# Large SBUF pages of a one-core encoder layer moved to multiples of 128 bytes

## The chip, the cores and the metric

The kernel runs on one core of one Trainium2 chip. The metric is the device time of one execution in microseconds. Three runs of the kernel before took 1744.45 to 1746.06 us, 1745.98 in the median. The core has a matrix engine (TensorE, called PE in the profile, with its weight loads shown apart as PEld), a vector engine (VectorE, DVE), an activation engine (ScalarE, ACT), a general engine (GpSimd, POOL) and a queue engine (SyncE, SP) that here only issues DMA transfers. SBUF is the memory on the core from which the engines read: 128 partitions, each with its own run of bytes. A tile of shape [128, n] lies at the same byte address in every partition. PSUM is where PE writes its results.

## The reference, cut to what matters

One layer (DEPTH = 1) of a bidirectional encoder over 1024 positions of 1024 features, all in float32:

```python
h = _rmsnorm(x, attn_norm_w[layer])
proj = jnp.einsum("bsd,de->bse", h, w_in)         # 8192 columns: GLU input, q, v, z_f, z_b, og, g_a, g_b
a = jax.nn.glu(glu_in); a = _dwconv_centred(a, dw_w, dw_b)     # 31 taps
a = jnp.einsum("bsc,cd->bsd", jax.nn.silu(_layernorm(a, ln_w, ln_b)), pw_w)
o = _bi_hgrn2(q, v, z_f, z_b, lb[0], lb[1])       # gated scan in both directions, 8 heads of 128
bmix = jnp.einsum("bse,ed->bsd", norm(o) * jax.nn.silu(og), o_w)
y = jax.nn.sigmoid(g_a) * a + jax.nn.sigmoid(g_b) * bmix
x = x + jnp.einsum("bsd,de->bse", y, w_out[layer])
gate, val = jnp.split(jnp.einsum("bsd,df->bsf", _rmsnorm(x, ffn_norm_w), w_up), 2)
x = x + jnp.einsum("bsf,fd->bsd", jax.nn.silu(_dwconv_centred(gate, ...)) * val, w_down)   # 2816 wide, 3 taps
return _rmsnorm(x, final_norm_w)
```

Most of the arithmetic is in the large products: with `w_in`, `hgrn_o_w`, `w_out`, `ffn_w_up` and `ffn_w_down`.

## The kernel before

**Matmuls.** All large products are made of one kind of matmul: a weight block of 128x128 stays in the array while 512 columns of activations move through it (the moving operand is a page of 128x512 elements, 2048 bytes in each partition). To keep float32 precision, every operand is split into a high part in the rounded type fp32r and a low part (line 124: ACT casts the high part, then DVE subtracts it for the low part). A product is then three matmuls, on lines 148 to 150: high by high, high by low, low by high. Each matmul has its own weight load. Products with `w_in` and with `ffn_w_up` save an eighth of the work: two output columns by two halves of the sequence are computed with seven products in place of eight (`pair_job`, in the order 1, 2, 6, 7, 5, 4, 3), which need sums and differences of the activations (made once) and of the weights. A pair of columns is 7 products of 12 matmuls, 84 in all.

**Weight sums.** In `pair_job` the weight rows come into a page `wr` (two buffers), the other columns into `sw`. Where no stored sums exist, GpSimd issues DMA transfers that add in flight: into `sw` from memory (`G.dma_start(o, a, accum_op=ALU.add)`, line 301), then from `sw` into `wr`, then within `wr`. In the feed-forward `sw` has one buffer, so its next load (lines 374 and 375, issued on SP's queue) waits until it has been read. The first three feed-forward columns use sums stored earlier and do without.

**Order.** PE's instructions run in the order in which the program writes them. The other engines' instructions are put in order by a planner with a cost model, except a few that are pinned. Side work is interleaved by hand with counts of pieces (a piece is six matmuls), for example 1.67 pieces of projection behind each tap of the 31-tap convolution on DVE (line 1037).

**Stages**, by the profile's time: norm and gated input to 87 us; the convolution on DVE beside input projections to about 335; the rest of the projections and the layer norm to about 478; the scan of eight heads beside the remaining projections to about 870; output of the scan and `w_out` to about 1088; the up projection of the feed-forward (22 columns) to about 1493; the down projection to 1697; the final norm and the stores.

**Where the tiles lie.** Pools of tiles are stacked in SBUF: a pool that is released gives its space to the next. Within a pool tiles follow each other, each rounded up to 32 bytes. Below all lie 16512 bytes and the pool of constants, which ends at 19488. So the start of a page depends on everything below it. These are the starts modulo 128 before the change (first page in brackets; all pages of a row have the same remainder unless two are given):

| pool | tiles | start mod 128 before |
|---|---|---|
| main (from 19488) | `tm` `wr` `wp` `hx` `ev` | 32 |
| gp0 (123936), p0, p1 (140832) | `gl` `ch`; `xt` `xn`; `su` `hy` `sw` `w` `wq` `ca` | 32 |
| heads (123936) | `none`, 64 bytes | 32 |
| heads (124000) | `q` `f` `kG` `zi` `qF` `D` `A` `tb` | 96 |
| heads (193568), behind three `Tt` of 64 bytes | `Sf` `Sb` `S` `v` `kT` `jk` `og` | 32 |
| fw (123936), p4 (148512) | `h` (named `h7`) `rs` `sw`; `mg` `x2` `xq` | 32 |
| fu (148512) | two `gp` of 4104 bytes | 32 and 64 |
| fu (156768) | `ft` `w` (named `w4`) `su` `wq` `hy` | 96 |
| fd (123936), fs (194848), fy | `xr` `gx`; `sr` `wq` `su`; `y` | 32 |

`ident`, the identity matrix that the transposes use as moving operand, starts at 16512, a multiple of 128. In the up projection the seven products take their operands from pages of different remainders: products 1, 2 and 6 move `hx` pages (32) against `wp` weights (32); product 7 moves `h` pages (32) and product 5 `hx` pages (32) against `wq` weights (96); product 4 moves `hy` (96) against `wq` (96); product 3 moves `hy` (96) against `wp` (32).

## Time and profile before

| what | us |
|---|---|
| median of three runs | 1745.98 |
| the profiled execution | 1742.35 |
| its span, first to last instruction | 1740.5 |
| PE busy in the span | 1711.8 (98%) |
| DVE busy | 1254.2 (72%) |
| ACT busy | 828.0 (48%) |
| DMA, mean rate over the span | 177 GB/s |

The granted clock of PE was 0.998 of full speed over the execution. A row of the profile's groups reads: line, engine, operation, tile written and tiles read, shapes, count, then the group's busy time, the mean duration of one in ns, and the idle time of its engine just before them with what ended it. Matmuls overlap each other, so the mean duration of one (some 390 ns) is not what one costs; the distance from start to start is. Windows cut the span into stretches and give each engine's busy time and its number of instructions in each.

### The profile page before, as it was taken

What the parts mean: (1) busy time and instruction counts of PE and PEld (TensorE: products, weight loads), DVE (VectorE), ACT (ScalarE), POOL (GpSimd) and SP (SyncE); (2) the same over time, 40 slices, a digit from 0 to 9 for tenths busy, and PEclk for the clock granted to TensorE, in tenths of its full rate; (3) what the DMA queues carried; (4) which work ended last, traced back from release to release, by engine and by line L of the source; (5) the groups of instructions that cost most, each with busy time, mean ns of one, the idle gap of its engine ahead of it and who ended that gap; (6) DMA issues with size and microseconds to landing.
All of it is one profiled execution on the core that took longest, in us unless ns stands there. A gap on an engine that the chain in (4) does not pass through costs nothing. (4 is left out here: it accounts for less than half of the span.)

```text
span 1740.5 us, 30439 instructions
## 1 busy us (share of the span) xinstructions
PE 1711.8 (98%) x11806; PEld 1409.4 (81%) x11806; DVE 1254.2 (72%) x1919; ACT 828.0 (48%) x1544; POOL 170.2 (10%) x184
## 2 busy tenths in 40 slices
PE   8999999999999999999999999999999999999997
PEld 6878888887888888888878887888888888888775
DVE  4599999746678888787556467667767776657864
ACT  7444433334476777776342245444334434443333
POOL 2211111100000000000000002011111111000110
PEclk9999999999999999999999999999999999999999
DMA  8768888855663444446589466577777776783842
GB/s 284 241 169 186 198 189 195 210 162 159 211 202 108 126 131 126 126 120 202 176 257 329 140 206 193 146 146 167 157 167 160 180 170 152 230 264 109 202 91 97
DMA packets 343750, 308.26 MB, mean 177 GB/s; under 512 B 25262, under 2 KB 255798, under 8 KB 343606
## 3 DMA queue, kind: packets, MB, share of 16 engines
q1 hardware_dynamic: 289590, 267.51, 49.0%
q0 software_dynamic: 44800, 37.76, 15.2%
q10 hardware_dynamic: 9216, 1.05, 0.4%
q8 instruction: 92, 1.51, 0.4%
q14 instruction: 52, 0.43, 0.1%
HBM read 201.40 MB, written 87.03 MB: 166 GB/s over the span
## 5 line engine op out<-in xcount | busy, mean ns | idle before, releaser
L148 PE MATMUL mm<-hx,wp 128*128 128x512 f32 x1068 | 427.3, 400 | 3.3 <-ACT tm L849 1.4
L150 PE MATMUL mm<-hx,wp 128*128 128x512 f32 x1068 | 417.1, 391 | 0.9 <-DVE wp L124 0.9
L149 PE MATMUL mm<-hx,wp 128*128 128x512 f32 x1068 | 416.6, 390 | 0.4 <-DVE hx L124 0.4
L124 ACT CAST wp<-wr 128x1024 fp32r<-128x1024 f32 (+2 forms) x147 | 147.2, 1002 | 258.6 <-PE mm L149 112.5
L148 PEld LDWEIGHTS mm<-hx,wp 128*128 128x128 f32 x1068 | 200.6, 188 | 46.7 <-DVE ev L798 2.2
L150 PEld LDWEIGHTS mm<-hx,wp 128*128 128x128 f32 x1068 | 200.4, 188 | 45.1 <-DVE wp L124 2.4
L149 PEld LDWEIGHTS mm<-hx,wp 128*128 128x128 f32 x1068 | 200.8, 188 | 40.5 <-DVE hx L124 1.2
L124 DVE TENSOR_TENSOR wp<-wr,wp 128x1024 fp32r<-128x1024 f32 (+2 forms) x145 | 169.5, 1170 | 67.3 <-ACT wp L124 61.0
L1037 DVE SCALAR_TENSOR_TENSOR acc<-gl,v_b,acc 128x1024 f32<-128x1024 f32 x120 | 149.2, 1282 | 0.4
L1142 DVE TENSOR_TENSOR qF<-qF,tb 128x512 f32<-128x512 f32 x96 | 65.1, 686 | 21.0 <-ACT A L1174 20.9
L439 ACT COPY su<-mm 128x512 f32<-128x512 f32 x82 | 47.5, 579 | 59.2 <-PE mm L150 58.9
L124 ACT CAST wq<-sw 128x1024 fp32r<-128x1024 f32 x41 | 43.1, 1052 | 59.5 <-PE mm L149 44.6
L148 PE MATMUL tr<-hx,wp 128*128 128x512 f32 x180 | 70.5, 392 | 0.0
L150 PE MATMUL tr<-hx,wp 128*128 128x512 f32 x180 | 70.1, 389 | 0.0
L149 PE MATMUL tr<-hx,wp 128*128 128x512 f32 x180 | 70.0, 389 | 0.0
L1634 DVE SCALAR_TENSOR_TENSOR tm<-gp,v_a,tm 128x512 f32<-128x512 f32 x88 | 66.0, 750 | 3.9 <-ACT tm L1632 2.0
L1142 DVE TENSOR_TENSOR kG<-kG,tb 128x512 f32<-128x512 f32 x96 | 65.3, 686 | 3.7 <-PE sc L1279 3.6
L148 PE MATMUL mm<-hy,wp 128*128 128x512 f32 x164 | 64.5, 393 | 0.0
L148 PE MATMUL sc<-hy,wq 128*128 128x512 f32 x164 | 64.3, 392 | 0.0
L149 PE MATMUL mm<-hy,wp 128*128 128x512 f32 x164 | 64.3, 392 | 0.0
L150 PE MATMUL sc<-hy,wq 128*128 128x512 f32 x164 | 64.2, 391 | 0.0
L149 PE MATMUL sc<-hy,wq 128*128 128x512 f32 x164 | 63.8, 389 | 0.0
(372 smaller groups left out, 3577.6 us busy)
## 6 DMA issues: line engine op xcount, KB each, us to landing
wr<-in_w_in_dram SPq DMA_DIRECT2D x48, 512.0 KB, 4.7
wr<-in_ffn_w_up_dram SPq DMA_DIRECT2D x22, 512.0 KB, 4.0
sw<-in_w_in_dram SPq DMA_DIRECT2D x38, 256.0 KB
d_g<-ft SPq DMA_DIRECT2D x38, 256.0 KB, 3.4
sw<-in_ffn_w_up_dram SPq DMA_DIRECT2D x38, 256.0 KB, 4.4
sw<-in_ffn_w_up_dram POOLq DMA_DIRECT2D x19, 512.0 KB, 8.1
wr<-sw POOLq DMA_DIRECT2D x32, 256.0 KB, 3.6
wr<-wr POOLq DMA_DIRECT2D x32, 256.0 KB, 4.0
```

Of the source, the lines that this page charges most:

```text
L124: parts = A.copy(hi, src), eng.tensor_tensor(lo, src, hi.bitcast(F32), op=ALU.subtract)
L148: T.matmul(acc, whi[:, k, :], ahi, start=first, stop=False, skip_group_check=again)
L149: T.matmul(acc, whi[:, k, :], alo, start=False, stop=False, skip_group_check=again)
L150: T.matmul(acc, wlo[:, k, :], ahi, start=False, stop=last, skip_group_check=again)
L439: A.copy(t, acc)
L1037: V.scalar_tensor_tensor(acc, g[:, k : k + S], tap(k), acc, op0=ALU.mult, op1=ALU.add)
L1142: V.tensor_tensor(o, a, b, op=op)
L1634: V.scalar_tensor_tensor(c, g[:, o + k : o + k + H], vec("fdw", k * NF + j), c, op0=ALU.mult, op1=ALU.add,)
```

## The change

A constant `ALIGN = 128` is added and four places in the allocation change; no instruction is added or taken out. An unused tile of 96 bytes behind `ones_m` moves everything above it. `none` becomes 128 bytes long, of which the first 64 are used as before. `Tt` gets a fourth buffer. The two `gp` tiles of the feed-forward become 4224 bytes long, and the code uses the same 1026 elements of each as before.

```diff
+ALIGN = 128
...
     ones_m = cp.tile([P, P], F32, name="ones_m")
+    cp.tile([P, ALIGN // 4 - 8], F32, name="offset")
...
-    none = hp.tile([P, 32], mybir.dt.bfloat16, name="none")
+    none = hp.tile([P, ALIGN // 2], mybir.dt.bfloat16, name="none")[:, :32]
...
-        Tt = hp.tile([P, 2, 2, 4], F32, tag="Tt", name=nm("Tt"), bufs=3)
+        Tt = hp.tile([P, 2, 2, 4], F32, tag="Tt", name=nm("Tt"), bufs=4)
...
-    gp += [fu.tile([P, S + 2], F32, name=f"gp{i}") for i in range(2)]
+    gp += [fu.tile([P, S + ALIGN // 4], F32, name=f"gp{i}") for i in range(2)]
```

Worked through the table above: main starts at 19584 and everything below the scan's and the feed-forward's own tiles moves by 96; the `q` to `tb` tiles of heads move by 160 to 124160; those behind `Tt` by 224 to 193792; the second `gp` by 192 and the `ft` to `hy` tiles by 288 to 157056. All pages of the table then start at a multiple of 128. Modulo 256 the pages of main and most others start at 128 (before: 32), those of heads up to `S` at 0 (before: 96 or 32). The pools keep their places relative to each other but for these shifts, so nearly every tile overlaps the same tiles of the pools before it. The differences: `f` of heads no longer reaches into the last 64 bytes of the first `gl` page; most pages of `fs` overlap one `hy` page less; a few pages of `mg`, `ft` and `hy` lie over one tile more or less of heads, which was released long before.

## The prediction

> **What bounds the kernel now.** First the head of the page: TensorE (PE) is busy for 98% of the span, the chain that ended last runs mostly through PE, and the largest group of all is one kind of matmul, 128x512 in fp32r.

> ```profile
> span 1740.5 us, 30439 instructions
> PE 1711.8 (98%) x11806; PEld 1409.4 (81%) x11806; DVE 1254.2 (72%) x1919; ACT 828.0 (48%) x1544; POOL 170.2 (10%) x184
> PE 43%; DMA 2%; issue 2%; DVE 1%; ACT 1%; POOL 0%; SPq 0%; POOLq 0%; ACTq 0%; DVEq 0%
> L148 PE MATMUL mm<-hx,wp 128*128 128x512 f32 x1068 | 427.3, 400 | 3.3 <-ACT tm L849 1.4
> ```

> The durations there overlap, so what one matmul costs is read from starts. Second view: busy time and counts over chosen stretches (columns: length; PE, PEld, DVE, ACT and POOL busy with counts; clock; DMA share; GB/s).

> ```profile
> 958.00:1026.00 68.00, 68.00 (x301) 56.31 (x301) 34.76 (x48) 23.78 (x35) 0.00 (x0) 1.00 0.52 161
> 1100.00:1485.60 385.60, 385.60 (x1681) 315.52 (x1680) 275.37 (x366) 156.43 (x221) 63.33 (x57) 1.00 0.73 163
> ```

> The first stretch has 300 matmuls from start to start in 68.00 us, 226.67 ns each. The second has twenty columns of the feed-forward (84 matmuls each, seven products of 12): 19.28 us a column, 229.5 ns each. Third view: the order of instructions on PE in one column, of which I show the first matmul of products 6, 7, 5, 4, 3 and of the next column.

> ```profile
> 1268.96 0.39 PE L148 MATMUL mm<-hx,wp 128*128 128x512 f32 x1
> 1271.68 0.40 PE L148 MATMUL sc<-h,wq 128*128 128x512 f32 x1
> 1274.48 0.40 PE L148 MATMUL mm<-hx,wq 128*128 128x512 f32 x1
> 1277.28 0.39 PE L148 MATMUL sc<-hy,wq 128*128 128x512 f32 x1
> 1280.04 0.39 PE L148 MATMUL mm<-hy,wp 128*128 128x512 f32 x1
> 1282.79 0.39 PE L148 MATMUL mm<-hx,wp 128*128 128x512 f32 x1
> ```

> Differences over 12: product 6 takes 226.7 ns a matmul, 7 and 5 take 233.3, 4 takes 230.0, 3 takes 229.2. The instructions are the same; what differs is where the pages start. Behind the last multiple of 128 bytes, `hx`, `h` and `wp` start at 32, `wq` and `hy` of this stage at 96. So (moving, weights) at (32, 32) is the fastest pair, (32, 96) the slowest: start addresses cost PE time here.

> The sizes fit one unit. 226.67 ns is 17 times 13.33; 233.33 is 17.5 times; the column of 19.28 us is 1446.0 times 13.33 against 84 x 17 = 1428. A moving page of 2048 bytes that starts at 32 or 96 touches 17 lines of 128 bytes; one that starts at a multiple touches 16. My reading: PE fetches lines of 128 bytes at 13.33 ns each, and a weight page that starts at another place than the moving page now and then costs one more.

> **The change part by part.** No instruction is added or removed; the tile `offset` (96 bytes) has no accesses. Every large page moves to a multiple of 128.

> *Matmuls.* By that reading a matmul goes from 17 lines to 16, 213.3 ns, plus what a turn costs. For the turn the trace has transposes, whose moving operand `ident` starts at a multiple of 128 already, beside fp32 matmuls whose moving operand starts at 32:

> ```profile
> 569.04 0.60 PE L1318 MATMUL tr<-ident,kG 128*128 128x128 f32 x4
> 569.48 0.60 PE L1318 MATMUL mm<-ident,kG 128*128 128x128 f32 x4
> 571.31 1.05 PE L1327 MATMUL sc<-v,kT 128*128 128x128 f32 x8
> 572.20 1.06 PE L1327 MATMUL mm<-v,kT 128*128 128x128 f32 x8
> ```

> 0.44 us for four is 110 ns, 0.89 for eight is 111. Eight units would be 106.7, so a turn is near 3 ns (with rows in steps of 10 ns, no better than that). I take 216 for the aligned matmul. The ends are 213.3 (no turn) and 226.67 (the 17 units are no lines and stay). I take the end near 216 because the extra line explains the 17, the halves and the 1446 at once.

> [...]

> How many there are, by stage (first all instructions, then those of L148, which issues one in three):

> ```profile
> 0.00:87.00 87.00, 79.99 (x376) 64.68 (x377) 44.23 (x67) 50.71 (x83) 19.87 (x33) 1.00 0.81 262
> 87.00:335.00 248.00, 245.43 (x1080) 202.21 (x1080) 241.03 (x259) 97.45 (x136) 40.52 (x41) 1.00 0.81 189
> 335.00:478.00 143.00, 142.22 (x627) 116.04 (x626) 81.60 (x109) 58.82 (x91) 6.07 (x8) 1.00 0.59 181
> 478.00:870.00 392.00, 389.07 (x5946) 326.78 (x5946) 309.43 (x670) 270.56 (x595) 12.97 (x14) 1.00 0.48 147
> 870.00:1088.00 218.00, 215.78 (x963) 176.27 (x962) 130.05 (x184) 86.45 (x145) 11.69 (x14) 1.00 0.71 225
> 1088.00:1493.00 405.00, 405.00 (x1766) 331.42 (x1765) 291.42 (x389) 168.10 (x240) 63.33 (x57) 1.00 0.72 163
> 1493.00:1697.00 204.00, 202.78 (x899) 166.32 (x898) 136.94 (x211) 79.12 (x162) 13.76 (x16) 1.00 0.65 175
> ```

> ```profile
> 0.00:87.00 87.00, 30.80 (x76) 14.28 (x76) 1.00 0.81 262
> 87.00:335.00 248.00, 140.25 (x360) 67.46 (x360) 1.00 0.81 189
> 335.00:478.00 143.00, 80.05 (x201) 37.66 (x201) 1.00 0.59 181
> 478.00:870.00 392.00, 140.23 (x339) 63.52 (x338) 1.00 0.48 147
> 870.00:1088.00 218.00, 119.07 (x305) 57.08 (x304) 1.00 0.71 225
> 1088.00:1493.00 405.00, 230.68 (x589) 110.41 (x588) 1.00 0.72 163
> 1493.00:1697.00 204.00, 114.49 (x293) 54.92 (x293) 1.00 0.65 175
> ```

> Three times the count, times 10.67 ns (13.5 in the feed-forward), is what PE alone could save: 2.4, 11.5, 6.4, 10.9, 9.8, 23.9 and 9.4 us, with 1.2 for the rest: 75.6 us. In each stage I then ask who takes over:
> - 0 to 87: PE is busy 80 of 87 us and waits for first loads. I take 1.
> - 87 to 335, the depthwise convolution: VectorE (DVE) is busy 241.0 of 248 us. It becomes the bound at once; its idle 7.0 us is the most there is. I take 4 of 11.5.
> - 335 to 478: DVE 57%, nobody near: 6.
> - 478 to 870, the scan: DVE 79%, ACT 69%, chains between the engines: 9 of 10.9.
> - 870 to 1088: some waits for loads: 8 of 9.8.
> - 1088 to 1493, the feed-forward's up projection: a loop of transfers stands behind PE:

> ```profile
> 1287.20 1.58 POOL L301 DMA_DIRECT2D sw<-in_ffn_w_up_dram  x1 [6.49 <-issue]
> 1296.01 0.89 POOL L301 DMA_DIRECT2D wr<-sw  x1 [7.23 <-DVE tm L1643]
> 1299.71 0.37 SPq L374 DMA_DIRECT2D sw<-in_ffn_w_up_dram  x1
> 1305.67 1.58 POOL L301 DMA_DIRECT2D sw<-in_ffn_w_up_dram  x1 [4.95 <-DMA sw<-in_ffn_w_up_dram]
> SPq L374 <- DMA wr<-sw: 46.2, 12, 7.2
> ```

> `sw` has one buffer: loaded, added into (1287.20 to 1296.01), added from into `wr` (to 1299.71, when the next load is issued), loaded again (to 1305.67). This turn took 18.47 us without PE; SP waited for it in 12 columns. A faster PE would want 84 x 216 = 18.14. Nineteen columns go this way (the first three use stored sums). I take 18.8 for them: 19 x 0.48 + 3 x 1.14 = 12.5, and 11 for safety with the first column.
> - 1493 to 1697: 8 of 9.4. The rest: 1.

> Sum: 1 + 4 + 6 + 9 + 8 + 11 + 8 + 1 = 48 us.

> *Other engines.* The convolution's taps read `gl` at 32 + 4k behind a multiple of 128, so every offset in steps of 4 occurs, one of them 0:

> ```profile
> L1037 DVE SCALAR_TENSOR_TENSOR acc<-gl,v_b,acc x120: 1274/1283/1287, 90.8 to 328.5; 128x1024 f32<-128x1024 f32 x120
> ```

> 1% from the least to the most: DVE gains nothing, and I take nothing for ACT and POOL, which I bound by the same 1%; both lie beside PE.

> *Waits.* The fourth `Tt` buffer only lets the head's totals wait for an older head: nothing, hidden by a whole head of scan work. If that cover were gone it would be one DVE step. Page `f` no longer overlaps the last 64 bytes of the first `gl` page, and in the down projection most pages of `fs` overlap one `hy` page less: waits go, none comes. No DMA moves to another queue.

> *Transfers.* Every DMA into or out of SBUF has a new start. No row shows the price of that alone; the nearest is the load of `sw` above, 5.96 us from issue to use. I take nothing, and treat a loss as a rival.

> The profiled execution took 1742.35 us, 3.6 below the median 1745.98 of the three runs; 1742.35 - 48 = 1694.4, and by the median 1698.

> **The rivals.**
> 1. *The feed-forward follows PE after all*: the loop's waits shorten with everything else. 12 us more: 1686.
> 2. *More is held back*: no gain in the up projection (the mean turn of the loop is the column's 19.28 already) and little in the scan: about 32 us: 1714.
> 3. *The 17th unit is not a line* but a fixed turn of these matmuls. Then only the mixed pairs go to 226.67: 18 units or 0.24 us a column, 22 columns, 5.3 us, and some 3 elsewhere: 1738. For it: the trace has no 128x512 fp32r matmul with an aligned moving page. Against: 17.5 and 17.25 in place of 17 depend on starts 64 bytes apart, so a unit of 128 bytes exists.
> 4. *Nothing changes*: 1746. The rows of products 6 and 7 speak against it. [...]
> 5. *Slower: the two reads of PE meet*. If a moving and a weight page that both start on a line collided as (32, 96) does, all matmuls (some 6600 by the counts above) would take 233.3 ns. Now 1767 take 229.5 and the rest 226.67, 227.4 in the mean: 39 us more, 1785. It decides against the change from a mean of 228 up. For it: (96, 96) takes 230.0 though both starts agree. Against it: (32, 32) agrees too and is the fastest.
> 6. *Slower: the transfers stretch.* If the loop's transfers took, say, a sixth more, its turn of 18.47 us would be 21.6, and 19 columns would lose 2.3 us each, 44 us, against 37 won elsewhere: about 1753. It decides from a turn of about 21.2 us. Against it: no row shows such a price. [...]

> **How the numbers follow.** Chances: the forecast 0.47, rival 1 0.12, 2 0.11, 3 0.18, 4 0.03, 5 0.04, 6 0.05. The time is that of the first, 1698. The range must hold rival 3, so it goes to 1742; below it reaches 1668, where all 75.6 us are won and the turn is half of mine. That leaves out rivals 4 to 6 and the ends of the others, 0.17. The likeliest case's own range is 1688 to 1708. A measurement tells 0.2%, 3.5 us, from no change: faster 0.87 (the forecast and rivals 1 to 3, less 0.01 of rival 3), same 0.05, slower 0.08.

> **What would show it.** In the changed kernel the stretch with `mg` pages should show 300 matmuls in 64.8 us, not 68.0; products 6, 7, 5, 4, 3 should all take the same; the convolution's stage should show DVE above 98% and PE waiting for `wp`; the up projection should show PE waiting for `wp` behind DMA `wr<-wr`. The prediction is wrong if the 300 still take 68.0 (rival 3), more (5), or if the loop's turn is longer (6).

## The result, and the profile after

The changed kernel takes 1741.3 us in the median, the kernel before 1746.0 us in the same measurement: a ratio of 0.9975 with a 95% interval of 0.9965 to 0.9985, 4.7 us or a quarter of a per cent faster (20 executions of each). The forecast was 1698 us. The profiled execution took 1740.57 us (before 1742.35), its span 1738.7 us.

Lines behind the edits have moved: 148 to 150 are now 149 to 151, 124 is 125, 301 is 302, 374 is 375, 439 is 440. The head of the page of the changed kernel, its chain, and the largest group:

```profile
span 1738.7 us, 30440 instructions
PE 1708.0 (98%) x11806; PEld 1408.5 (81%) x11806; DVE 1252.1 (72%) x1919; ACT 828.3 (48%) x1544; POOL 170.1 (10%) x184
PE 40%; DMA 4%; issue 2%; DVE 2%; ACT 1%; POOL 0%; SPq 0%; POOLq 0%; ACTq 0%; DVEq 0%
L149 PE MATMUL mm<-hx,wp 128*128 128x512 f32 x1068 | 427.6, 400 | 4.9 <-ACT su L440 2.1
```

PE is busy 3.8 us less (1711.8 before), the span is only 1.8 us shorter, the chain has 3 points less of PE and 2 more of DMA, and the largest group now waits for ACT. The same two stretches as before (columns as in the prediction):

```profile
958.00:1026.00 68.00, 68.00 (x302) 56.33 (x301) 34.74 (x48) 24.10 (x36) 0.00 (x0) 1.00 0.53 166
1100.00:1485.60 385.60, 383.31 (x1686) 315.50 (x1685) 274.52 (x367) 157.54 (x224) 63.33 (x57) 1.00 0.74 164
```

The first stretch, all pages now at multiples of 128, still holds 300 matmuls in 68.00 us: 226.67 ns each, not 216. The second, the up projection, was filled by PE before and held 1681 matmuls; now it holds 1686 and PE is idle for 2.3 us of it. One column there, the first matmul of products 6, 7, 5, 4, 3 and of the next column:

```profile
1266.15 0.39 PE L149 MATMUL mm<-hx,wp 128*128 128x512 f32 x1
1268.88 0.39 PE L149 MATMUL sc<-h,wq 128*128 128x512 f32 x1
1271.60 0.39 PE L149 MATMUL mm<-hx,wq 128*128 128x512 f32 x1
1274.32 0.39 PE L149 MATMUL sc<-hy,wq 128*128 128x512 f32 x1
1277.04 0.39 PE L149 MATMUL mm<-hy,wp 128*128 128x512 f32 x1
1279.76 0.39 PE L149 MATMUL mm<-hx,wp 128*128 128x512 f32 x1
```

The differences are 2.72 or 2.73 us, 226.7 ns a matmul; products 7, 5, 4 and 3 have lost their extra. So the time of the mixed pairs (products whose two pages start at different places) is won in this column, the hoped 11 ns of all others is not. What the up projection then waits for, as total, times and longest:

```profile
SPq L375 <- DMA wr<-sw: 54.5, 16, 8.3
```

```profile
PE mm L149 <- ACT su L440: 2.1, 2, 1.6
```

And a place where it does so, from the order of instructions on POOL, ACT and PE:

```profile
1299.00 0.86 POOL L302 DMA_DIRECT2D wr<-wr  x1 [3.86 <-DMA wr<-sw]
1304.41 1.04 ACT L125 CAST wp<-wr 128x1024 fp32r<-128x1024 f32 x1 [9.51 <-PE tr L151]
1305.37 0.58 ACT L440 COPY su<-mm 128x512 f32<-128x512 f32 x1
1306.00 0.50 PE L149 MATMUL mm<-hx,wp 128*128 128x512 f32 x1 [1.60 <-ACT su L440]
```

GpSimd's second in-flight addition into `wr` is issued at 1299.00. ACT sits in front of the cast of those sums until 1304.41 (the profile names PE for it, but in the same trace the addition lands at 1304.32, just before the cast). The copy of product 1's bank is queued behind the cast on ACT, and PE needs that copy before product 6 may use the bank: it stands idle for 1.60 us at 1306.00. The wait for the loop of `sw` is thus paid through ACT's queue. SP's own wait for `wr<-sw` came 12 times and 46.2 us before, 16 times and 54.5 us now.

### The profile page after: what moved, and what is told of

The parts are those of the page before. It is cut to its first block, busy times and chain, and to the rows that moved or that the text cites. A ratio compares the mean times of both kernels' runs of the same rounds, so it can differ in the third digit from the quotient of the medians.

```text
span 1738.7 us, 30440 instructions
## 1 busy us (share of the span) xinstructions
PE 1708.0 (98%) x11806; PEld 1408.5 (81%) x11806; DVE 1252.1 (72%) x1919; ACT 828.3 (48%) x1544; POOL 170.1 (10%) x184
## 3 DMA queue, kind: packets, MB, share of 16 engines
q10 hardware_dynamic: 9216, 1.05, 0.4%
## 5 line engine op out<-in xcount | busy, mean ns | idle before, releaser
L149 PE MATMUL mm<-hy,wp 128*128 128x512 f32 x164 | 64.2, 391 | 0.0
L150 PE MATMUL mm<-hy,wp 128*128 128x512 f32 x164 | 63.8, 389 | 0.0
L150 PE MATMUL sc<-hy,wq 128*128 128x512 f32 x164 | 63.8, 389 | 0.0
L151 PE MATMUL mm<-hy,wp 128*128 128x512 f32 x164 | 63.8, 389 | 0.0
L151 PE MATMUL sc<-hy,wq 128*128 128x512 f32 x164 | 63.8, 389 | 0.0
```

The costliest lines, as they stand in the source:

```text
L149: T.matmul(acc, whi[:, k, :], ahi, start=first, stop=False, skip_group_check=again)
L150: T.matmul(acc, whi[:, k, :], alo, start=False, stop=False, skip_group_check=again)
L151: T.matmul(acc, wlo[:, k, :], ahi, start=False, stop=last, skip_group_check=again)
```

## Experiments: what in the start addresses costs time

The forecast spoke of lines of 128 bytes. The trace after says that a start at a multiple of 128 does nothing for a matmul whose pages were alike already. Theory A: what costs is that the moving page and the weight page of a matmul start at different places behind a multiple of 128; rival B: the multiple itself helps, in part of the matmuls or in the accesses of DVE and the DMAs.

**All pages at 32, and all at 96.**

```diff
-    cp.tile([P, ALIGN // 4 - 8], F32, name="offset")      # all at 32
...
-    cp.tile([P, ALIGN // 4 - 8], F32, name="offset")
+    cp.tile([P, 16], F32, name="offset")                  # all at 96
```

> The changed kernel without its `offset` tile: the paddings stay, so every large page starts at 32 behind a multiple of 128, and all 6636 matmuls of 512 fp32r columns have equal starts (32, 32). Theory A (what costs is that the moving page and the weight page of a matmul start at different places modulo 128; the place itself costs nothing): as the changed kernel, 1741.3 us, +-1.5, with products 7, 5, 4 and 3 of the feed-forward at 226.7 ns a matmul. Rival B (the multiple of 128 itself is what helps): 1745 or more, as before. Rival C (the gain is DVE's or the DMAs', by their own alignment): also nearer 1746.

> The changed kernel with 64 bytes in place of 96 for `offset`: every large page starts at 96 behind a multiple of 128, all 6636 matmuls have (96, 96). Theory A (only a difference of the starts costs): 1741.3 us +-1.5. Rival B2 (a page at 96 costs by itself, which the kernel before seems to show: its product 4, moving 96 and weights 96, took 230.0 ns against 226.7 for (32, 32)): 6636 x 3.4 ns = 22.6 us more, about 1764; half of it where something else bounds.

Measured, against 1743.8 us for the kernel before in the same measurement: 1741.5 us with all pages at 32 (ratio 0.9984, 0.9973 to 0.9996) and 1741.0 us with all at 96 (0.9972, 0.9962 to 0.9982). The three alignments give the same gain within their intervals, and products 7, 5, 4 and 3 take 226.7 ns a matmul in both traces. The place is not what counts; rivals B, B2 and C fall.

**Aligned pages, but the mixed pairs kept.**

```diff
     ones_m = cp.tile([P, P], F32, name="ones_m")
+    cp.tile([P, 24], F32, name="offset")
```

> The kernel before with the `offset` tile alone and none of the paddings: pages of the main pool at multiples of 128, those of the feed-forward's own pool and of the scan at 64; 528 matmuls have (0, 64), 264 (64, 64), 264 (64, 0), as many as were mixed before. Theory A: no gain, 1746 us +-1.5, products 7 and 5 still at 233 ns, 3 at 229. Rival B (aligned pages gain by themselves): most of the change's gain, since 5580 matmuls are now at (0, 0): 1742.

Measured: 1743.4 us (ratio 0.9995, 0.9985 to 1.0004), no gain, with 5580 of the 6636 matmuls at multiples of 128. The column of this kernel, products 6, 7, 5, 4, 3 and the next:

```profile
1270.08 0.39 PE L148 MATMUL mm<-hx,wp 128*128 128x512 f32 x1
1272.80 0.40 PE L148 MATMUL sc<-h,wq 128*128 128x512 f32 x1
1275.60 0.40 PE L148 MATMUL mm<-hx,wq 128*128 128x512 f32 x1
1278.39 0.39 PE L148 MATMUL sc<-hy,wq 128*128 128x512 f32 x1
1281.16 0.39 PE L148 MATMUL mm<-hy,wp 128*128 128x512 f32 x1
1283.90 0.39 PE L148 MATMUL mm<-hx,wp 128*128 128x512 f32 x1
```

Products 7 and 5 take 233 ns a matmul (2.80 and 2.79 us over 12) and 4 and 3 some 231 and 228, as in the kernel before.

**One edit of the four.** The `gp` tiles alone put the feed-forward's own pages where the main pool's are, all at 32:

```diff
-    gp += [fu.tile([P, S + 2], F32, name=f"gp{i}") for i in range(2)]
+    gp += [fu.tile([P, S + 32], F32, name=f"gp{i}") for i in range(2)]
```

> The kernel before with one of the change's four edits alone: the two `gp` tiles are 4224 bytes long. All pages stay at 32 behind a multiple of 128, but the feed-forward's `ft` to `hy` pages now have the remainder of the main pool modulo 256 too: all 6636 matmuls have a difference of 0. Theory A2: this edit is the whole gain, so as the changed kernel, 0.2 to 0.3% below the kernel before (3 to 5 us), products 7, 5, 4 and 3 at 226.7 ns. Rival (the multiples of 128 in the scan or in DVE's and the DMAs' accesses give part of it): no gain or half of it.

Measured: 1741.6 us against 1745.5 (ratio 0.9977, 0.9963 to 0.9991). That is the whole gain of the change, within the interval; the offset tile, `none` and `Tt` add nothing that can be measured.

**How far apart, and in which sense.** Four kernels displace one kind of page in the changed kernel, with unused tiles ahead of and behind it (`shift` and `back`):

```diff
+    mp.tile([P, 32], F32, name="shift")     # ahead of the first hx: 128 bytes
...
+    mp.tile([P, 32], F32, name="back")      # behind ev
```

This is the kernel with `hx` 128 away. The others differ only in the place and the sizes: 64 and 64 bytes around `hx` and `ev`, 32 and 224 around the same, and 64 and 192 around `wp`. In three of them the unused bytes add up to 256, so that all else keeps its place modulo 256. In the one with 64 and 64 they add up to 128, and the pools above main lie 128 further as well: there `mg` and `hy` pages move 128 away from `wp` too.

> The changed kernel with two unused tiles of 64 bytes, one ahead of the `hx` pages and one behind the `ev` pages: `hx` and `ev` start at 64 behind a multiple of 128, everything else stays at a multiple. 4536 matmuls then have moving 64 against weights 0. Theory A with the price that the feed-forward's products 7 and 5 showed before (6.67 ns a matmul): 4536 x 6.67 ns = 30 us more, less what DVE hides in the convolution, so 1763 to 1772. With the price of product 3 (2.2 ns): 1751. If the difference of starts is no cause: 1741.

> The changed kernel with two unused tiles of 128 bytes, one ahead of the `hx` pages and one behind the `ev` pages: every large page still starts at a multiple of 128, but `hx` at 0 modulo 256 and all else at 128 modulo 256. 4536 matmuls move `hx` against weights 128 away modulo 256. Theory A (a difference modulo 128 costs): no change against the changed kernel, 1741 us. Theory A2, formed after the run with `hx` at 64, where pairs with equal remainders modulo 128 but 128 apart modulo 256 took 232.4 ns a matmul (a difference modulo 256 costs): 4536 x 5.7 ns = 26 us more, less what the feed-forward's loop and the first stage hide: 1758 to 1767.

> The changed kernel with unused tiles of 64 bytes ahead of the `wp` pages and 192 bytes behind them: only `wp` moves, by 64, all else keeps its place modulo 256. 4728 matmuls move pages that start 64 short of their weights (192 ahead modulo 256), the sense of products 7 and 5 before; with `hx` at 64 it was the other sense and the pairs took 230.2 ns in the mean. Theory A2 with a price by the signed difference (64 ahead about 229 to 230 ns, 192 ahead 233.3): 4728 x 6.6 ns = 31 us more, 1765 to 1773. Rival: the price goes by the distance without sign, 3.3 ns: 4728 x 3.3 = 16 us more, about 1757.

> The changed kernel with unused tiles of 32 bytes ahead of the `hx` pages and 224 bytes behind the `ev` pages: only `hx` and `ev` move, by 32. 4536 matmuls move pages 32 ahead of their weights. If every difference modulo 256 costs, between 0 and the 230 ns of a difference of 64: at most 1757. If only differences of 64 and more cost: 1741, at 226.7 ns.

Measured, all slower than the kernel before, though nothing but addresses differs:

| displaced | us | ratio to before | 95% interval |
|---|---|---|---|
| `hx` by 64 | 1758.2 | 1.0073 | 1.0056 to 1.0089 |
| `hx` by 128 | 1758.2 | 1.0082 | 1.0066 to 1.0099 |
| `wp` by 64 | 1762.8 | 1.0104 | 1.0090 to 1.0118 |
| `hx` by 32 | 1761.8 | 1.0087 | 1.0054 to 1.0119 |

Of the four expectations only that for `hx` by 128 (1758 to 1767) holds in its number. `wp` by 64 came out below its 1765 to 1773, `hx` by 64 between its two prices, and `hx` by 32 above the 1757 that was to be the most. The times alone don't tell prices apart; the products do.

The kernel with `hx` 128 away decides between A and A2. All its large pages start at multiples of 128, and yet it is 0.8% slower than before. Its column, products 1, 2, 6, 7, 5, 4, 3 and the next:

```profile
1273.44 0.40 PE L149 MATMUL mm<-hx,wp 128*128 128x512 f32 x1
1276.24 0.40 PE L149 MATMUL tr<-hx,wp 128*128 128x512 f32 x1
1279.04 0.40 PE L149 MATMUL mm<-hx,wp 128*128 128x512 f32 x1
1281.84 0.39 PE L149 MATMUL sc<-h,wq 128*128 128x512 f32 x1
1284.57 0.40 PE L149 MATMUL mm<-hx,wq 128*128 128x512 f32 x1
1287.36 0.39 PE L149 MATMUL sc<-hy,wq 128*128 128x512 f32 x1
1290.10 0.39 PE L149 MATMUL mm<-hy,wp 128*128 128x512 f32 x1
1292.82 0.40 PE L149 MATMUL mm<-hx,wp 128*128 128x512 f32 x1
```

The four products that move `hx` take 2.79 to 2.80 us, 233 ns a matmul; the others, whose pages agree modulo 256, take 2.72 to 2.74. So it is the difference modulo 256 that costs. Product 6 and its successor in the kernels with `hx` at 32, `wp` at 64 and `hx` at 64:

```profile
1281.52 0.39 PE L149 MATMUL mm<-hx,wp 128*128 128x512 f32 x1
1284.32 0.40 PE L149 MATMUL sc<-h,wq 128*128 128x512 f32 x1
```

```profile
1283.67 0.40 PE L149 MATMUL mm<-hx,wp 128*128 128x512 f32 x1
1286.47 0.39 PE L149 MATMUL sc<-h,wq 128*128 128x512 f32 x1
```

```profile
1279.77 0.39 PE L149 MATMUL mm<-hx,wp 128*128 128x512 f32 x1
1282.53 0.40 PE L149 MATMUL sc<-h,wq 128*128 128x512 f32 x1
```

2.80 us each for moving pages that start 32 ahead of their weights or 64 short of them, 2.76 for 64 ahead. Over all matmuls of these traces, moving start less weight start modulo 256, from start to start: 0 gives 227.0 ns (`hx` against `wp` in the changed kernel outside the scan), 32 gives 233.3, 64 gives 228.9 (product 3 before) to 230.3 (`hx` at 64), 128 gives 232.4 (`mg` against `wp` in the kernel with `hx` at 64) to 233.0 (`hx` at 128), 192 gives 233.3 (products 7 and 5 before, and `wp` at 64). Why 64 ahead is cheaper than 32 ahead no run shows. The price goes by the signed difference, since 192 (64 short) costs 6.6 ns and 64 costs 2.2 to 3.6; the rival without sign falls. The kernels' times rose by less than count times price: by the expectation for `wp`, 31 us; measured, some 22 over the changed kernel by the two ratios (1.0104 against 0.9975). Part of that is waits PE had anyway: in the kernel with `hx` by 128, PE fills the whole feed-forward stretch again (383.31 in the changed kernel).

```profile
1100.00:1485.60 385.60, 385.60 (x1673) 313.82 (x1672) 275.63 (x363) 156.21 (x221) 63.36 (x57) 1.00 0.73 162
```

## Experiments: the 13.3 ns that stayed

The prediction took a matmul of 226.7 ns for 17 units of 13.33 ns and called one of them a seventeenth line. The probe cuts matmuls and changes the type:

```diff
-    o_jobs += [std_job(o_cols(i), NH, bm_of, merge(i)) for i in range(2, ND)]
+    CUTS = [((0, 256), (256, 512)), ((0, 384), (384, 512))]
+    o_jobs += [std_job(o_cols(i), NH, bm_of, merge(i), cuts=CUTS) for i in range(2, ND)]
...
-                std_job(w_cols(w_out, 0, ND, i * P), ND, lambda k, half: mg[k][half], x2_evac(i))
+                std_job(w_cols(w_out, 0, ND, i * P), ND, lambda k, half: mg[k][half], x2_evac(i), bf=True)
```

> A probe of what the 13.3 ns above 512 x 0.4167 = 213.3 ns are. In the output projection the matmuls with 512 moving columns are cut in two, 256 + 256 for the first half of the sequence and 384 + 128 for the second; in the product with `w_out` all operands are bf16 copies in place of the split fp32r (so part of the computation has another precision, and the low parts are left out). Theory F (a fixed turn of 13.3 ns a matmul): 120.0 ns for 256, 173.3 for 384, 66.7 for 128 where the weight load does not hold it. Theory G (a share of the columns, 17 for 16, as in the prediction's lines): 113.3, 170.0, 56.7. For bf16 with 512 columns: 226.7 if the turn belongs to every matmul of this size, 213.3 to 216 if it belongs to fp32r.

A matmul of 256 columns, the first of 384 behind it, the first ones of 128; then a stretch that holds only bf16 matmuls of 512 columns:

```profile
966.41 0.28 PE L263 MATMUL mm<-hx,wp 128*128 128x256 f32 x1
970.37 0.34 PE L263 MATMUL mm<-hx,wp 128*128 128x384 f32 x1
974.53 0.22 PE L263 MATMUL mm<-hx,wp 128*128 128x128 f32 x1
974.59 0.27 PE L264 MATMUL mm<-hx,wp 128*128 128x128 f32 x1
975.49 0.27 PE L263 MATMUL mm<-hx,wp 128*128 128x128 f32 x1
...
992.00:1064.00 72.00, 72.00 (x335) 32.63 (x334) 39.38 (x61) 33.92 (x52) 0.00 (x0) 1.00 0.65 208
```

33 matmuls of 256 columns lie between 966.41 and 970.37: 120.0 ns each. 24 of 384 lie between there and 974.53: 173.3. With 226.7 for 512 that is 13.3 ns and 0.4167 ns a column, as theory F says: a fixed turn of these fp32r matmuls at 256, 384 and 512 columns. Theory G would have 113.3 and 170.0. In bf16 the same 512 columns take 215.8 ns from start to start (mean of 332 in this stretch), so if a column costs the same 0.4167 ns the turn is near 2.5 ns there (an estimate: 215.8 less 213.3), and the 13.3 belong to fp32r. Whether the turn is the matmul's own or that of changing its weights no run shows: every matmul here has its own weight load, of 188 ns in fp32r and 98 in bf16.

128 columns take 0.90 us for 8, 112 ns, far above the 66.7 that the fixed turn would give; the cause (the weight load, or another) was not told apart.

## Experiments: where the feed-forward's share went

Theory D: the loop of the one `sw` page was hidden by PE before, and takes back most of the 5.3 us that the mixed pairs cost. Two kernels without the in-flight additions, one of the kernel before and one of the changed one:

```diff
-            stored=sums_of(d_us[n], ND // 2) if n < len(d_us) else None,
+            stored=sums_of(d_us[n % 3], ND // 2),
```

> The kernel before with the weight sums of the first three feed-forward columns read from memory for all 22 columns: the in-flight additions and their loop of `sw` are gone, and the weight sums of the later columns are the wrong ones, so the output isn't the layer's. Theory D (the loop of transfers hid behind PE before, and takes back most of what the mixed pairs cost after the change): 1743.8 us, no change against the kernel before, 229.5 ns a matmul in the up projection.

> The changed kernel with the same edit (stored sums for all 22 columns, wrong for the later ones). Theory D: the up projection at 226.7 ns a matmul without waits, 22 x 84 x 2.85 ns = 5.3 us less than the kernel before in that stage, so about 1737.5, some 3 to 4 us below the changed kernel. Rival E (the mixed pairs' 5 us were mostly there for the taking and something else holds the end): 1741, as the changed kernel.

Measured against 1744.4 us: 1743.5 us without the loop and without the change (ratio 0.9993, 0.9984 to 1.0002), 1737.3 us without the loop and with the change (0.9959, 0.9945 to 0.9973). The loop cost the kernel before nothing that can be measured. Without it the change is worth 6.2 us; with it, 4.7 us in the median. The profiled executions show the up projection alone: from the first product 7 of its first column to that of its last, 21 columns, it took 407.6 us before, with and without the loop, 402.7 with the change and without the loop, and 406.6 with both. So equal starts are worth 4.9 us there, and the loop left 1.0 of them. The same stretch in the two kernels, before first:

```profile
1100.00:1485.60 385.60, 385.60 (x1682) 315.55 (x1681) 277.10 (x365) 156.69 (x222) 0.00 (x0) 1.00 0.41 137
```

```profile
1100.00:1485.60 385.60, 385.60 (x1703) 319.40 (x1702) 281.74 (x373) 160.26 (x228) 0.00 (x0) 1.00 0.42 140
```

1682 matmuls against 1681 with the loop, and 1703 against 1686: with equal starts PE could do 21 or 22 more, the loop left 5 of them.

This is one execution, and what the up projection takes changes from one to the next. The profiled executions with all pages at 32, with all at 96 and with the `gp` tiles alone, which are 1.2 to 3.7 us above their medians, took 408.4, 408.4 and 408.9 us for these 21 columns: more than the kernel before, although their matmuls are as fast as the changed kernel's. And the loop can reach PE without the change too: the profiled execution with the `offset` tile alone, 5.4 us above its median, has stops of PE in this stage and took 413.0. So no run says how the 4.7 us of the median divide.

**Two pages for `sw`.** The loop can be opened without leaving anything out:

```diff
-            fw,
+            up if n % 2 else fw,
             up,
             evac,
+            su=3,
...
-        t = page(fu, "ft", 8)
+        t = page(fu, "ft", 7)
```

(and `ft` with 7 buffers in its two other places).

> The changed kernel, with the odd columns of the feed-forward keeping their `sw` page in the feed-forward's own pool, so that two columns' pages are in flight; room for it from one `ft` page (8 to 7) and one `su` page (4 to 3) less. Nothing is left out. Theory D (the loop of the one `sw` page holds back what the matmuls gained): most of the 4.0 us that the stored sums gave, 1737 to 1739. Rival: the next link holds just as well (the in-flight additions on POOL's queue behind each other, or the page taken from `ft` or `su` is missed): 1741 or more.

Measured: 1737.0 us against 1745.5 (ratio 0.9945, 0.9925 to 0.9964), 8.6 us faster than the kernel before and 4.6 below the one with the `gp` tiles alone in the same measurement. The stretch, and ACT's waits for `wp` in the feed-forward:

```profile
1100.00:1485.60 385.60, 385.60 (x1702) 319.27 (x1702) 281.68 (x373) 160.84 (x228) 61.70 (x56) 1.00 0.73 164
```

```profile
ACT wp L125 <- PE mm L150: 83.4, 19, 4.4
...
ACT wp L125 <- DMA wr<-wr: 4.7, 1, 4.7
```

1702 matmuls, as many as without the additions, and 402.7 us for the 21 columns: PE never waits there. ACT now waits for PE to free `wp` pages, 19 times, and once for the addition into `wr`; in the changed kernel it was 16 times and 104.1 us for the addition. The additions are the same ones; they come earlier, by a mean turn of 19.0 us from load to load in place of 19.4. The time is the 1737 to 1739 that theory D gave, not its rival's 1741 or more, with nothing left out. How much the loop takes is less sure: 4.6 of 8.6 us here, where the interval of the 8.6 reaches from 6 to 13 us, and 1.5 of 6.2 us by the medians with the stored sums.

## Why the prediction was wrong in size and right in direction

- **The failed step** is the first one of the sum: "By that reading a matmul goes from 17 lines to 16". The 17 units of 13.33 ns were 16 units for 512 columns and one fixed turn of a fp32r matmul; it was priced as something that an aligned start removes. The probe shows 120.0 and 173.3 ns for 256 and 384 columns, and the 300 matmuls still take 68.00 us. All that was summed from it (1 + 4 + 6 + 9 + 8 + 8 + 1 = 37 us outside the up projection) was not there: PE at 98% stayed at 226.7 ns a matmul, and the convolution's stage, where DVE was to become the bound, takes 247.9 us by the starts of its matmuls before and after. None of the other stages outside the up projection changed by more than 0.6 us between the two profiled executions. The 11 us of the up projection rested on the same step.
- **The turn taken from the transposes** (near 3 ns, from 110 ns for 128 columns) could not bear on 512 columns. 128 columns take 112 ns in the probe, whose pages all agree, where the fixed turn alone would give 66.7: a length at which the turn does not show. The prediction priced by rows that this turn does not explain.
- **The unit that explained too much.** 17, 17.5 and 1446 times 13.33 fitted, and the halves were read as lines fetched now and then. The price goes by the difference of the two starts modulo 256, and in a product it is a mean over a pattern (228.9 for 64 ahead, 233.3 for 64 short). The one pair that spoke for rival 5, (96, 96) at 230.0, agreed in its starts and still was slow. In the trace before, its twelve matmuls run 228, 229, 234, 236, 224, 231, 236, 228, 232, 231, 227, 226 ns in the median of 20 columns, which differ by 2 ns at most: a settling after the mixed product 5 ahead of it. In the kernel with all pages at 96 the same pair takes 227 throughout, so rival 5 had no ground.
- **Rival 3 is what happened**, at 1741 in place of its 1738. Its 5.3 us for the mixed pairs of 22 columns were right (4.9 us for 21 of them with the loop gone). Its "some 3 elsewhere" were not there, and the loop took part of the rest.
- **The loop** was the right thing to fear: it stood close behind PE, and a faster PE met it, through ACT's cast and the copy queued behind it. Its turn was mis-sized. The 18.47 us came from one column; over all its turns the loop has a mean of 19.4 us, before and after, as its first and last loads show (18 turns apart, before and then after):

```profile
1110.60 1.63 POOL L301 DMA_DIRECT2D sw<-in_ffn_w_up_dram  x1 [28.54 <-DVE gp L1665]
1460.23 1.60 POOL L301 DMA_DIRECT2D sw<-in_ffn_w_up_dram  x1 [4.84 <-DMA sw<-in_ffn_w_up_dram]
```

```profile
1109.37 1.63 POOL L302 DMA_DIRECT2D sw<-in_ffn_w_up_dram  x1 [28.35 <-DVE gp L1667]
1458.57 1.60 POOL L302 DMA_DIRECT2D sw<-in_ffn_w_up_dram  x1 [4.99 <-DMA sw<-in_ffn_w_up_dram]
```

That is 19.42 and 19.40 us, with single turns from 17.4 to 21.3, above the 18.8 that the prediction took and above the 19.04 that 84 matmuls of 226.67 ns need. With two pages for `sw` the mean turn fell to 19.02 us. Rival 2 came close to this part ("the mean turn of the loop is the column's 19.28 already").
- **Rival 6, stretched transfers**, did not come. DMA issues in the up projection (count, KB each, median from issue to landing), before and then after:

```profile
sw<-in_ffn_w_up_dram POOLq DMA_DIRECT2D x19, 512.0 KB, 8.1
wr<-wr POOLq DMA_DIRECT2D x19, 256.0 KB, 4.5
```

```profile
sw<-in_ffn_w_up_dram POOLq DMA_DIRECT2D x19, 512.0 KB, 8.0
wr<-wr POOLq DMA_DIRECT2D x19, 256.0 KB, 4.9
```

The 512 KB load took 8.1 us before and 8.0 after; in the kernel with the `gp` tiles alone, whose pages stay at 32, it took 7.9. The transfer within `wr` took 0.4 us more, but not by its start: it took 5.0 us in that kernel with its pages at 32, and 3.3 in the one with two `sw` pages, at multiples of 128.
- **The range** held the time, because it reached to rival 3; the likeliest case's own range, 1688 to 1708, did not. Its lower end does not follow from its own terms: all 75.6 us won give 1670, and half the turn (1.3 ns for some 6600 matmuls) would take it to about 1662, not 1668.

## What to carry to other kernels

Compare the time from one matmul to the next, product by product, before believing in a unit; a length that varies (256, 384, 512 columns) told a fixed turn from a price per column in one run here (120.0, 173.3 and 226.7 ns). Where a weight block and the activations that move through it lie in different pools, and the matmuls are like these (fp32r, 512 columns), give both the same start modulo 256: 226.7 ns here, against 229 to 233 with different starts. The alignment itself was worth nothing here (ratio 0.9984 with all pages at 32, 0.9975 at multiples of 128, alike within their intervals), and a multiple of 128 was no safeguard (1758.2 us with `hx` 128 away). And when PE gains a few microseconds in a stage with a one-buffer loop close behind it, open the loop in the same change: here the loop left 1.0 of 4.9 us in the profiled executions, and the opened one took 1737.0 us.
